# Down projection of a feed-forward layer: two halves over 22 row blocks, or seven half-size products over 11

## Chip, cores and metric

One Trainium2 chip, one of its cores. The metric is the device time of one launch in microseconds (us). Names of engines: PE multiplies matrices and loads its stationary operand (PEld), DVE works on vectors, ACT evaluates functions and copies, POOL is the general engine, which also issues transfers by a queue of its own, and SP issues most transfers. Sums of products stand in PSUM banks of 128 x 512 numbers, everything else that an engine reads in SBUF. DRAM is the memory that transfers read and write.

## Reference

Two decoder layers on 512 tokens of width 1024, all in f32. Each has a mixer (layer 0: forgetting attention and a short convolution; layer 1: a gated linear recurrence, RG-LRU), a cross attention into 256 memory rows, and a gated feed-forward part. Cut to what the change touches:

```python
D_FF = 2816
def swiglu(h, w_gu, w_down):
    g, u = jnp.split(h @ w_gu, 2, axis=-1)
    return (jax.nn.silu(g) * u) @ w_down          # (512 x 2816) @ (2816 x 1024)
for layer in range(2):
    ...                                            # mixer, cross attention
    h = rmsnorm(x, g_ffn_pre[layer])
    y = swiglu(h, w_ffn_gu[layer], w_ffn_down[layer])
    x = x + rmsnorm(y, g_ffn_post[layer])
```

## The kernel before

Every f32 operand of PE is split in two parts of type fp32r, hi (a rounded copy, made by ACT) and lo (the rest, made by DVE: `split_out`), and a product is three products: hi x hi, hi x lo, lo x hi. Tokens stand in four tiles `t` of 128 rows, `x[t]`.

Weights come as tiles `st` of 512 KB from DRAM by SP's queue (pool `wst`, 4 buffers) and are split into `wh` and `wl` (pools `whi` and `wlo`, 4 buffers each). A load waits until DVE has split the tile that had its buffer; a split waits until PE is done with the tile that had the `wh` buffer. So the loads run about eight tiles ahead of PE. Larger arrays are groups of 128 x 2048 numbers (pool `gpool`, 14 buffers).

The feed-forward part `ffn` has three stages. A first pair of columns is made by `ws_gemm_split`, while `hook` ends the sub-layer before (row norms of tiles 2 and 3, transposes). Then `Winograd.stream` makes the gate and up products as seven half-size products for each chunk of 256 columns, 20 chunks. Each pair of chunks gives two row blocks of y = silu(g) * u, which POOL stores in DRAM (`put_y`) from a tile of `wst`. Last comes the down projection (`OutProj` with `nk` = 22 row blocks of 128 of `w_ffn_down`). `half0` makes output columns 0 to 511 for all four token tiles, `half1` columns 512 to 1023; y is loaded back in groups (`load_y`) and split by `parts`, and the last eight row blocks of `half1` run tile by tile, so that `chain` (sum of squares, `rstd` with a power on POOL, gain, add to `x`) and the next row norm of one tile lie beside the products of the next.

Within `Winograd.stream` the programs of PE, DVE, ACT and POOL are the order of the code. In the rest only PE's is, and a scheduler orders the other engines' instructions. SP's is always the scheduler's. Each engine runs its own program strictly in order.

Of the kernel before, what the change touches and what calls it, by code (L numbers as in the profile page):

```python
# [15 lines left out]
P = 128  # L16
# [9 lines left out]
LEAD = 2  # L26
# [8 lines left out]
WHI = 4  # L35
# [7 lines left out]
def trunk_kernel(ctx: ExitStack, tc: tile.TileContext, a: dict, out: bass.AP):  # L43
# [32 lines left out]
    def f(ap):  # L76
        return ap.bitcast(F32)
# [39 lines left out]
    def load_raw(w, k0, nk, c0, c):  # L117
        st = wst.tile([P, nk, c], F32, tag="st", name="st")
        nc.sync.dma_start(
            out=st, in_=w.rearrange("(k p) n -> p k n", p=P)[:, k0:k0 + nk, c0:c0 + c]  # L120
        )
        return st
# [4 lines left out]
    def load_rows(w, k0, n, c0):  # L127
# [5 lines left out]
        return hi, lo  # L133

# [65 lines left out]
    def rstd(st):  # L200
# [9 lines left out]
        nc.gpsimd.tensor_tensor(out=st[:, 4:5], in0=st[:, 3:4], in1=nhalf, op=ALU.pow)  # L210
# [307 lines left out]
    class OutProj:  # L518
        def __init__(self, w, y, nk, g_post, g_pre, hT, first=bankA, second=bankB, final=False):
# [6 lines left out]
            self.ready = {}  # L526
            self.ahead = self.gate = None
# [10 lines left out]
        def half0_steps(self, ks, first, last):  # L538
# [5 lines left out]
            for n, k in enumerate(ks):  # L544
                wt = self.ready.pop(k) if k in self.ready else load_w(self.w, k, 2, 0, 512)
                if self.ahead:
                    for k2 in ks[n + LEAD:n + LEAD + 1]:
                        self.ahead(k2)
# [76 lines left out]

        def run(self):
            self.half0(range(0, self.nk, 2), True, True)
            self.half1()
# [42 lines left out]
    def memory_kv(layer, vhi, vlo, between):  # L671
# [5 lines left out]
        for c in range(4):  # L677
# [8 lines left out]
            split_out(ps, kh_[:, c, :], kl_[:, c, :])  # L686
        between()
# [16 lines left out]
    def cross(layer, hT, kv, proj, hTf):  # L704
# [6 lines left out]
        def q_head(h):  # L711
# [4 lines left out]
            qs[h] = q  # L716

# [76 lines left out]
    def ffn(layer, hT, prev, proj):  # L794
        w = a["w_ffn_gu"][layer]
        y = Feat([None] * NFF, [None] * NFF)

        y2 = dram.tile([P, NFF, 512], F32, name=f"y2_{layer}")
        yraw, yback = {}, {}
# [6 lines left out]
        def put_y(jp):  # L806
            nc.gpsimd.dma_start(out=y2[:, 2 * jp:2 * jp + 2, :], in_=yraw[jp])
# [31 lines left out]
        def load_y(i):  # L839
            n = min(4, NFF - 4 * i)  # L840
            yback[i] = f(group("yb"))
            nc.gpsimd.dma_start(out=yback[i][:, 0:n, :], in_=y2[:, 4 * i:4 * i + n, :])

        def parts(jp):
            if jp // 2 not in yback:
                load_y(jp // 2)
            yg = group("y")
            split_out(yback[jp // 2][:, jp % 2 * 2:jp % 2 * 2 + 2, :], yg[:, 0:2, :], yg[:, 2:4, :])
            for m in range(2):
                y.hi[2 * jp + m], y.lo[2 * jp + m] = yg[:, m, :], yg[:, 2 + m, :]  # L850

        def side(left):

            if left == 3:
                load_y(0)
            if left:
                return {}
            raw = [load_raw(proj.w, k, 2, 0, 512) for k in (0, 2)]
            for i in (1, 2):
                load_y(i)  # L860

            def weights(n):
                proj.ready[2 * n] = split_w(raw[n], 2, 512)

            return {"a": lambda: weights(0), "b": lambda: parts(0), "c": lambda: weights(1), "d": lambda: parts(1)}
# [7 lines left out]
        proj.y = y  # L873
        proj.ahead = lambda k: parts(k // 2)
        proj.run()


    def fox(proj):
# [136 lines left out]
        def qk_pairs(m0):  # L1015
# [12 lines left out]
            yield from ws_steps(w, m0 * P, hT, put_q)  # L1028
            yield from ws_steps(w, FOXW + m0 * P, hT, put_k)

# [73 lines left out]
        def conv(m0):  # L1104
# [30 lines left out]
            yield from ws_steps(w, base + FOXW, hT, put_c)  # L1135
            yield from ws_steps(w, base + 2 * FOXW, hT, put_u)
            yield from ws_steps(w, base, hT, put_b)

# [23 lines left out]
    def rglru(hT, prev, proj):  # L1162
# [70 lines left out]
        conv(0, b0)  # L1233
        conv(1, b1)
        conv(2, ws_gemm(w, D + 512, hT))
        gates(0)
        conv(3, ws_gemm(w, D + 768, hT))
        gates(1)
        gelu(0, ws_gemm(w, 0, hT))
        gates(2)  # L1240
        gelu(1, ws_gemm(w, 256, hT))
        gates(3)
        gelu(2, ws_gemm(w, 512, hT))
        gelu(3, ws_gemm(w, 768, hT))
# [55 lines left out]
```

## Time and profile before

| | |
|---|---|
| median of 3 runs | 1418.07 us (1417.96 to 1418.48) |
| the profiled execution, its own time | 1419.26 us |
| its span, first to last instruction | 1417.5 us, granted clock 0.997 |
| busy | PE 1406.5 us (99%), DVE 1013.9 (72%), ACT 663.6 (47%), POOL 55.9 (4%) |
| moved | 174.34 MB, mean 123 GB/s |
| down projection, first product | 622.6 us in layer 0, about 668.6 us later in layer 1 |

A line of groups reads: line of the code, engine, operation, output <- inputs with sizes, count, busy time and mean duration. A line of the timeline: start, duration, the same names, and in brackets how long the engine sat idle before it and what ended that. Starts are counted from the span's start.

### The profile page before, as it was taken

How to read it: one execution, taken by the hardware profiler on the slowest of the kernel's cores; microseconds unless marked ns; L12 is line 12 of the kernel's file. 1: busy time of each engine (PE TensorE's matmuls, PEld its weight loads, DVE VectorE, ACT ScalarE, POOL GpSimd, SP SyncE). 2: the span in 40 equal slices, each digit the busy share in tenths (PEclk: the TensorE clock that was granted, in tenths of full speed). 3: DMA queues.
4: the chain of work that ended last, by engine and by line, in shares of the span. 5: the costliest groups of instructions: out<-in, count | busy, mean ns of one | idle time of the engine just before them, and what ended most of it. 6: DMA issues, size and time to landing. Idle time of an engine off the chain costs nothing.

```text
span 1417.5 us, 21486 instructions
## 1 busy us (share of the span) xinstructions
PE 1406.5 (99%) x8564; PEld 1252.3 (88%) x8564; DVE 1013.9 (72%) x1623; ACT 663.6 (47%) x1069; POOL 55.9 (4%) x116
## 2 busy tenths in 40 slices
PE   8999999999999999999999999999999999999998
PEld 6778789888899999998889888988889999999886
DVE  5776777635689999992447898754478999998232
ACT  4354455433565444452334896543356444445130
POOL 1000001000000000010000000100000000000000
PEclk9999999999999999999999999999999999999999
DMA  5633152521234434373512336252023334347321
GB/s 175 190 89 99 56 184 83 194 90 45 68 117 144 148 121 138 131 266 120 164 52 82 104 93 198 97 178 89 31 80 114 129 125 147 122 144 272 104 74 60
DMA packets 124287, 174.34 MB, mean 123 GB/s; under 512 B 6725, under 2 KB 88721, under 8 KB 122906
## 3 DMA queue, kind: packets, MB, share of 16 engines
q1 hardware_dynamic: 114722, 140.92, 31.3%
q0 software_dynamic: 5568, 25.18, 4.8%
q10 hardware_dynamic: 3896, 6.86, 1.6%
q8 instruction: 67, 1.10, 0.3%
q14 instruction: 34, 0.28, 0.1%
HBM read 159.29 MB, written 13.65 MB: 122 GB/s over the span
## 4 chain that ended last, share of the span: by engine, by line
PE 99%; DMA 1%; ACT 0%; DVE 0%; DVEq 0%; POOLq 0%; issue 0%; SPq 0%; ACTq 0%
PE bA L299 14%; PE bA L301 14%; PE bA L300 14%; PE bB L300 6%; PE bB L299 6%; PE bB L301 6%; PE bA L534 5%; PE bA L536 5%; PE bA L535 5%; PE bB L535 5%; PE bB L534 5%; PE bB L536 5%; PE bA L905 2%; PE bB L283 1%; PE bA L697 1%; PE bA L699 1%
## 5 line engine op out<-in xcount | busy, mean ns | idle before, releaser
L510 DVE TENSOR_TENSOR wl<-st,wh 128x1024 fp32r<-128x1024 f32 x148 | 180.5, 1223 | 187.8 <-ACT wh L509 186.6
L509 ACT CAST wh<-st 128x1024 fp32r<-128x1024 f32 x148 | 155.3, 1051 | 214.4 <-PE bA L300 66.1
L299 PE MATMUL bA<-hTh,wh 128*128 128x512 f32 (+1 forms) x448 | 171.4, 383 | 0.0
L301 PE MATMUL bA<-hTh,wl 128*128 128x512 f32 (+1 forms) x448 | 168.0, 375 | 0.0
L300 PE MATMUL bA<-hTl,wh 128*128 128x512 f32 (+1 forms) x448 | 167.7, 374 | 0.0
L401 ACT CAST wg<-wr 128x1024 fp32r<-128x1024 f32 x80 | 83.6, 1046 | 49.1 <-DVE wr L430 37.6
L301 PEld LDWEIGHTS bA<-hTh,wl 128*128 128x128 f32 x448 | 84.3, 188 | 15.4
L402 DVE TENSOR_TENSOR wg<-wr,wg 128x1024 fp32r<-128x1024 f32 x80 | 97.4, 1217 | 0.0
L300 PEld LDWEIGHTS bA<-hTl,wh 128*128 128x128 f32 x448 | 84.5, 189 | 13.6
L299 PEld LDWEIGHTS bA<-hTh,wh 128*128 128x128 f32 x448 | 84.5, 189 | 13.5
L534 PE MATMUL bB<-wh,y 128*128 128x512 f32 x208 | 80.9, 389 | 0.0
L535 PE MATMUL bB<-wl,y 128*128 128x512 f32 x208 | 80.9, 389 | 0.0
L536 PE MATMUL bB<-wh,y 128*128 128x512 f32 x208 | 80.9, 389 | 0.0
L401 ACT CAST wh<-tt 128x1024 fp32r<-128x1024 f32 x40 | 42.1, 1052 | 61.2 <-DVE tt L430 61.2
L299 PE MATMUL bA<-hTq,wh 128*128 128x256 f32 x208 | 59.2, 284 | 0.0
L301 PE MATMUL bA<-hTq,wl 128*128 128x256 f32 x208 | 58.9, 283 | 0.0
L300 PE MATMUL bA<-hTq,wh 128*128 128x256 f32 x208 | 58.9, 283 | 0.0
L534 PE MATMUL bA<-wh,y 128*128 128x512 f32 x144 | 56.5, 392 | 0.0
L536 PE MATMUL bA<-wh,y 128*128 128x512 f32 x144 | 56.1, 390 | 0.0
L535 PE MATMUL bA<-wl,y 128*128 128x512 f32 x144 | 56.1, 389 | 0.0
L402 DVE TENSOR_TENSOR wl<-tt,wh 128x1024 fp32r<-128x1024 f32 x40 | 48.7, 1219 | 0.0
L534 PEld LDWEIGHTS bB<-wh,y 128*128 128x128 f32 x208 | 39.1, 188 | 8.1
(330 smaller groups left out, 4171.7 us busy)
## 6 DMA issues: line engine op xcount, KB each, us to landing
wr<-in_w_ffn_gu_dram SPq DMA_DIRECT2D x80, 512.0 KB, 4.6
st<-in_w_ffn_down_dram SPq DMA_DIRECT2D x44, 512.0 KB, 3.9
st<-in_w_xkv_dram SPq DMA_DIRECT2D x32, 512.0 KB, 4.6
st<-in_ab_w_in_dram SPq DMA_DIRECT2D x24, 512.0 KB, 3.8
y<-yr POOLq DMA_DIRECT2D x22, 512.0 KB, 3.9
yb<-y POOLq DMA_DIRECT2D x10, 1024.0 KB, 7.0
st<-in_w_xq_dram SPq DMA_DIRECT2D x16, 512.0 KB, 3.4
st<-in_w_xo_dram SPq DMA_DIRECT2D x16, 512.0 KB, 3.9
```

What stands on the lines that cost most here:

```text
L283: nc.tensor.transpose(out=ps[:, j * P:(j + 1) * P], in_=hs[hf][:, j * P:(j + 1) * P], identity=ident)
L299: nc.tensor.matmul(out=ps, lhsT=wh, rhs=xh, start=first, stop=False)
L300: nc.tensor.matmul(out=ps, lhsT=wh, rhs=xl, start=False, stop=False)
L301: nc.tensor.matmul(out=ps, lhsT=wl, rhs=xh, start=False, stop=last)
L401: return (lambda: nc.scalar.copy(out=to[0], in_=src), lambda: nc.vector.tensor_tensor(out=to[1], in0=src, in1=f(to[0]), op=ALU.subtract))
L402: lambda: nc.vector.tensor_tensor(out=to[1], in0=src, in1=f(to[0]), op=ALU.subtract))
L509: nc.scalar.copy(out=hi, in_=src)
L510: nc.vector.tensor_tensor(out=lo, in0=src, in1=f(hi), op=ALU.subtract)
L534: nc.tensor.matmul(out=ps, lhsT=yh, rhs=wh[:, kk, :], start=first, stop=False)
L535: nc.tensor.matmul(out=ps, lhsT=yh, rhs=wl[:, kk, :], start=False, stop=False)
L536: nc.tensor.matmul(out=ps, lhsT=yl, rhs=wh[:, kk, :], start=False, stop=last)
L905: nc.tensor.matmul(out=banks[t], lhsT=(hT.lo if c == "x" else hT.hi)[k][:, ts], rhs=(wl if c == "w" else wh)[:, kk, :], start=passes[t] == ...
```

## The change

The down projection becomes seven products of half the rows, half the depth and half the columns (a Strassen-Winograd form). The 22 row blocks are taken in pairs: even and odd blocks are the two halves of the depth (11 blocks each, `NJ`), columns 0 to 511 and 512 to 1023 the two halves of the width, tiles 0, 1 and 2, 3 the two halves of the tokens. Each product takes 11 row blocks x 2 token tiles x 3 matmuls of 512 columns, in 6 items (`NG`) of two blocks (the last of one).

The weight sums that four products need (`t1` to `t4`) are made in DRAM. For each layer 16 copies (SP) and 16 adding transfers (POOL, `accum_op`) of up to 786 KB are kept in the list `todo`, and `spend` issues the next few at places in the mixer, the cross attention and the gate and up stage: the copies in the mixer, eight adds in the cross attention, eight in the gate and up stage. The sums of y (`n1`, `n3`, `s2`, `n4`) are made in SBUF by DVE (`sub`), in place in the groups that hold y, one product ahead of their use; `part` splits the 512 numbers a partition that an item needs. The seven results are combined by DVE from the banks (`after`), and `finish` replaces `chain` and `next` in pieces that are set between the items. The whole down projection is now inside the stretch whose order on ACT, DVE and POOL is that of the code. The store of y writes runs of 256 numbers, where it wrote 1024.

```diff
+    todo = []
+    latest = {}
+    def spend(n=1):
+        for _ in range(min(n, len(todo))):
+            engine, step = todo.pop(0)
+            with tc.issue_after(latest[engine]):
+                latest[engine] = step().ins
...
+    class DownProj(OutProj):
+        NJ = NFF // 2
+        NG = (NFF + 3) // 4
+        A = {"a21": 0, "n3": 0, "a11": 1, "s2": 1, "n4": 1, "a22": 2, "n1": 2, "a12": 3}
+        ORDER = (("a11", "b11"), ("a22", "t4"), ("s2", "t2"), ("n3", "t3"), ("n1", "t1"), ("a12", "b21"), ("n4", "b22"))
+        RAW = {"b11": (0, 0), "b12": (0, 1), "b21": (1, 0), "b22": (1, 1)}
+            self.sums = {n: dram.tile([self.NJ * P, 512], F32, name=f"{n}_{layer}") for n in ("t1", "t2", "t3", "t4")}
+            self.y = dram.tile([P, self.NG, 4, 2, 256], F32, name=f"y_{layer}")
...
+            cuts = [(j, min(j + 3, self.NJ)) for j in range(0, self.NJ, 3)]
+            def step(to, frm, js, add):
+                if add:
+                    return nc.gpsimd.dma_start(out=self.rows(to, *js), in_=self.rows(frm, *js), accum_op=ALU.add)
+                return nc.sync.dma_start(out=self.rows(to, *js), in_=self.rows(frm, *js))
+            todo.extend(
+                ("pool" if add else "sp", lambda to=to, frm=frm, js=js, add=add: step(to, frm, js, add))
+                for add, pairs in ((False, (("t1", "b11"), ("t3", "b12"), ("t2", "b11"), ("t4", "b21"))),
+                                   (True, (("t3", "b22"), ("t1", "b12"), ("t2", "t3"), ("t4", "t2"))))
+                for to, frm in pairs for js in cuts
+            )
+        def put_y(self, jp, yr):
+            latest["pool"] = nc.gpsimd.dma_start(out=self.y[:, jp // 2, :, jp % 2, :],
+                                                 in_=yr.rearrange("p m (h c) -> p (m h) c", h=2)).ins
...
+        def sub(self, o, x, y, i):
+            r = self.raw[i]
+            nc.vector.tensor_tensor(out=r[:, self.A[o], :], in0=r[:, self.A[x], :], in1=r[:, self.A[y], :], op=ALU.subtract)
...
+            split_out(src, g[:, i % 2 * 2, 0:n], g[:, i % 2 * 2 + 1, 0:n])
+        def load_b(self, item):
+            (_, name), b = item
+            j0, j1 = 2 * b, min(2 * b + 2, self.NJ)
+            st = wst.tile([P, j1 - j0, 512], F32, tag="st", name="st")
+            nc.sync.dma_start(out=st, in_=self.rows(name, j0, j1))
+            return st
+        def split_b(self, s):
+            st = self.load_b(self.items[s])
+            self.wt[s] = split_w(st, st.shape[1], 512)
...
+        def mms(self, s, ts, banks):
+            (name, _), b = self.items[s]
+            wh, wl = self.wt[s]
+            for jj in range(wh.shape[1]):
+                j = 2 * b + jj
+                g = self.parts[name, b // 2]
+                for t in ts:
+                    cs = slice(jj * 256 + t * P, jj * 256 + t * P + P)
+                    yh, yl = g[:, b % 2 * 2, cs], g[:, b % 2 * 2 + 1, cs]
+                    first, last = j == 0, j == self.NJ - 1
+                    nc.tensor.matmul(out=banks[t], lhsT=yh, rhs=wh[:, jj, :], start=first, stop=False)
+                    nc.tensor.matmul(out=banks[t], lhsT=yh, rhs=wl[:, jj, :], start=False, stop=False)
+                    nc.tensor.matmul(out=banks[t], lhsT=yl, rhs=wh[:, jj, :], start=False, stop=last)
+        def finish(self, t, c):
+            st = self.st[t] = stats("post")
+            def square():
+                for hf in range(2):
+                    sumsq(c[hf], st[:, hf:hf + 1])
+            def gain(hf):
+                nc.vector.tensor_tensor(out=c[hf], in0=c[hf], in1=self.g_post[hf], op=ALU.mult)
...
+            return square, lambda: (gain(0), gain(1)), add, stats_x, root, scale
...
+            for i in range(len(self.raw), N):
+                self.load_y(i)
+            beside = {
+                0: lambda i: (self.part("a22", i), self.sub("n1", "a21", "a22", i)),
+                1: lambda i: (self.sub("n3", "a21", "a11", i), self.sub("s2", "a11", "n1", i), self.part("s2", i)),
+                2: lambda i: (self.part("n3", i), self.sub("n4", "a12", "s2", i)),
+                3: lambda i: self.part("n1", i),
+                4: lambda i: self.part("a12", i),
+                5: lambda i: self.part("n4", i),
+            }
+            p1, q, v, c21 = ([g[:, 2 * h + t, :] for t in range(2)] for g in (g1, g2) for h in range(2))
+                if x_ == 0:
+                    return [lambda t=t: nc.scalar.copy(out=p1[t], in_=bk[t]) for t in range(2)]
...
+                if x_ == 2:
+                    return [lambda t=t: tt(q[t], bk[t], p1[t], ALU.subtract) for t in range(2)]
+                if x_ == 3:
+                    return [lambda t=t: (tt(v[t], bk[t], q[t], ALU.add), tt(c21[t], C["p4"][t], v[t], ALU.subtract))
+                            for t in range(2)]
+                if x_ == 4:
+                    return [lambda t=t: (tt(v[t], bk[t], v[t], ALU.add), tt(q[t], bk[t], q[t], ALU.add)) for t in range(2)]
+                if x_ == 5:
+                    return [lambda t=t: tt(p1[t], bk[t], p1[t], ALU.add) for t in range(2)]
...
+            for t in range(2):
+                steps = self.finish(t, (c21[t], v[t]))
+                if self.final:
+                    steps = steps[:3]
+                else:
+                    steps += lambda t=t: self.transpose(t, bankB),
+                for n, fn in enumerate(steps):
+                    at = 5 * N + 1 + t + n
+                    extra.setdefault((at // N, at % N), []).append(fn)
...
+                if s + 2 < len(self.items) and s + 2 not in self.wt:
+                    self.split_b(s + 2)
+                if x_ == 0 and b + 2 < N:
+                    self.part("a11", b + 2)
+                if x_ in beside:
+                    beside[x_](b)
+                if b in (1, 2) and pend:
+                    pend.pop(0)()
+                for fn in extra.get((x_, b), ()):
+                    fn()
+                if x_ < 6 or b < N - WHI:
+                    self.mms(s, (0, 1), bk)
+                if b == N - 1 and x_ < 6:
+                    pend = after(x_, bk)
...
+            for t in range(2):
+                for s2 in range(len(self.items) - WHI, len(self.items)):
+                    self.mms(s2, (t,), bk)
+                tt(q[t], bk[t], q[t], ALU.add)
+                sq, ga, ad, st, ro, sc = self.finish(2 + t, (p1[t], q[t]))
+                sq()
+                ga()
+                for fn in last:
+                    fn()
+                ad()
+                if t == 0 and not self.final:
+                    st()
+                    ro()
+                    last = [sc]
...
+            proj.begin()
+            for i in (1, 2, 3):
+                proj.load_y(i)
+            return {"a": lambda: proj.split_b(0), "b": lambda: proj.part("a11", 0),
+                    "c": lambda: proj.split_b(1), "d": lambda: proj.part("a11", 1)}
...
```

Not shown: `spend` is called after each of four column groups of `memory_kv`, after each head of `cross`, at every second chunk of the gate and up stage (one step each), and twice at a time between the products of the mixers. The final stores of tiles 0 and 1 go to POOL's queue.

DVE's order where the gate and up stage of layer 0 ends and the down projection begins. Before (`wl` is the lo part of a weight tile, `y` that of two row blocks of y):

```order
L831 TENSOR_TENSOR yr_6336<-yr_6336,sw_6215 128x512
L510 TENSOR_TENSOR wl_6436<-st_6433,wh_6435 128x1024
L510 TENSOR_TENSOR y_6439<-yb_6251,y_6439 128x1024
L510 TENSOR_TENSOR wl_6469<-st_6466,wh_6468 128x1024
L510 TENSOR_TENSOR y_6472<-yb_6251,y_6472 128x1024
L510 TENSOR_TENSOR wl_6502<-st_6499,wh_6501 128x1024
L510 TENSOR_TENSOR y_6507<-yb_6505,y_6507 128x1024
L510 TENSOR_TENSOR y_6540<-yb_6505,y_6540 128x1024
L510 TENSOR_TENSOR y_6575<-yb_6573,y_6575 128x1024
```

Now, in the first product. `wl` is the weight tile two items ahead, `ya` the lo parts of the first and second product's y blocks, and the operation on `yb` alone the sum `n1`:

```order
L1044 TENSOR_TENSOR yr_6374<-yr_6374,sw_6251 128x512
L520 TENSOR_TENSOR wl_6428<-st_6425,wh_6427 128x1024
L520 TENSOR_TENSOR ya_6431<-yb_6283,ya_6431 128x512
L520 TENSOR_TENSOR ya_6434<-yb_5920,ya_6434 128x512
L685 TENSOR_TENSOR yb_5920<-yb_5920 128x512
L520 TENSOR_TENSOR wl_6453<-st_6450,wh_6452 128x1024
L520 TENSOR_TENSOR ya_6431<-yb_6285,ya_6431 128x512
L520 TENSOR_TENSOR ya_6434<-yb_6281,ya_6434 128x512
L685 TENSOR_TENSOR yb_6281<-yb_6281 128x512
L520 TENSOR_TENSOR wl_6476<-st_6473,wh_6475 128x1024
L520 TENSOR_TENSOR ya_6479<-yb_6415,ya_6479 128x512
```

Where DVE had one or two splits for each of 11 weight tiles of a half, each item now has four operations. In the second product these are a weight split, two sums (`n3` and `s2`, in one row), and the lo part of `s2`, whose hi part ACT makes from the sum just made:

```order
L685 TENSOR_TENSOR yb_6417<-yb_6417 128x256
L520 TENSOR_TENSOR wl_6563<-st_6560,wh_6562 128x1024
L685 TENSOR_TENSOR yb_5920<-yb_5920 128x512 x2
L520 TENSOR_TENSOR ya_6568<-yb_5920,ya_6568 128x512
L520 TENSOR_TENSOR wl_6586<-st_6583,wh_6585 128x1024
L685 TENSOR_TENSOR yb_6281<-yb_6281 128x512 x2
L520 TENSOR_TENSOR ya_6568<-yb_6281,ya_6568 128x512
L520 TENSOR_TENSOR wl_6609<-st_6606,wh_6608 128x1024
L685 TENSOR_TENSOR yb_6283<-yb_6283 128x512 x2
L520 TENSOR_TENSOR ya_6614<-yb_6283,ya_6614 128x512
```

POOL's order from the last row norm of layer 0's mixer on. Before, with the power operations of the norms (`post`, `pre`) and the first stores of y:

```order
L210 TENSOR_TENSOR pre_3543<-pre_3543,nhalf_108 128x1
L210 TENSOR_TENSOR post_3340<-post_3340,nhalf_108 128x1
L210 TENSOR_TENSOR pre_3646<-pre_3646,nhalf_108 128x1
L807 DMA y2_0_3577<-yr_3906 128x1024
L807 DMA y2_0_3577<-yr_4107 128x1024
L807 DMA y2_0_3577<-yr_4355 128x1024
L807 DMA y2_0_3577<-yr_4603 128x1024
L807 DMA y2_0_3577<-yr_4851 128x1024
```

Now eight adds stand behind the mixer's last norm and ahead of the cross attention's first, with nothing between them:

```order
L220 TENSOR_TENSOR pre_2208<-pre_2208,nhalf_108 128x1
L663 DMA t3_0_121<-in_w_ffn_down_dram 128x3x512 x3
L663 DMA t3_0_121<-in_w_ffn_down_dram 128x2x512
L663 DMA t1_0_119<-in_w_ffn_down_dram 128x3x512 x3
L663 DMA t1_0_119<-in_w_ffn_down_dram 128x2x512
L220 TENSOR_TENSOR post_3366<-post_3366,nhalf_108 128x1
L220 TENSOR_TENSOR pre_3456<-pre_3456,nhalf_108 128x1
L220 TENSOR_TENSOR post_3367<-post_3367,nhalf_108 128x1
L220 TENSOR_TENSOR pre_3514<-pre_3514,nhalf_108 128x1
L220 TENSOR_TENSOR post_3368<-post_3368,nhalf_108 128x1
```

130 lines of the change are left out of this document (90 added, 40 removed).

## Prediction

> **What bounds the kernel now.** I read the page's busy times first, then the chain of waits, then the stages one by one.
>
> ```profile
> PE 1406.5 (99%) x8564; PEld 1252.3 (88%) x8564; DVE 1013.9 (72%) x1623; ACT 663.6 (47%) x1069; POOL 55.9 (4%) x116
> PE 99%; DMA 1%; ACT 0%; DVE 0%; DVEq 0%; POOLq 0%; issue 0%; SPq 0%; ACTq 0%
> ```
>
> PE has work for 1406.5 of 1417.5 us, and the chain that ended last is PE almost throughout. So a matmul taken away is worth its full place in PE's row, until another engine or a transfer is late. The stages, by a table of windows (length, busy times, granted clock, DMA share, GB/s):
>
> ```profile
> core 0: us, PE busy (x) PEld busy (x) DVE busy (x) ACT busy (x) POOL busy (x), PEclk, DMA share, GB/s
> 64.00:130.00 66.00, 66.00 (x350) 52.12 (x349) 45.46 (x107) 32.43 (x66) 4.19 (x9) 1.00 0.36 104
> 240.00:264.00 24.00, 24.00 (x184) 23.12 (x183) 16.66 (x19) 12.29 (x16) 0.00 (x0) 1.00 0.61 199
> 264.00:300.00 36.00, 36.00 (x160) 29.81 (x159) 16.50 (x17) 13.80 (x17) 0.00 (x0) 1.00 0.46 146
> 424.00:604.00 180.00, 180.00 (x1501) 179.85 (x1500) 170.55 (x270) 81.81 (x107) 5.39 (x10) 1.00 0.40 135
> 622.00:640.00 18.00, 18.00 (x84) 15.02 (x83) 16.62 (x16) 9.94 (x11) 1.61 (x3) 1.00 0.88 318
> 640.00:680.00 40.00, 40.00 (x179) 33.10 (x178) 9.80 (x8) 7.62 (x8) 0.00 (x0) 1.00 0.31 99
> ```
>
> The reader sees a steady down projection (640 to 680) in which PE is full while DVE has 9.8 of 40 us and the transfers a third of their time: there is room for more vector work and more bytes. Its first 18 us are the opposite: DVE 16.6 of 18 us, DMA engines 0.88 busy at 318 GB/s.
>
> **What is removed: 132 matmuls.** Two halves x 22 blocks x 4 tiles x 3 = 528 matmuls a layer become 7 x 11 x 2 x 3 = 462, of the same form (stationary 128 x 128, 512 columns). A matmul's duration of 389 ns overlaps the next one, so the price is the distance of starts. The first row is from the list of y's readers, the other two are PE's timeline, 15 matmuls apart:
>
> ```profile
> L534 PE MATMUL bB<-wh,y x208: 389/389/396, 622.6 to 1350.4; 128*128 128x512 f32 x104
> 639.62 0.39 PE L534 MATMUL bB<-wh,y 128*128 128x512 f32 x1
> ...
> 643.02 0.39 PE L534 MATMUL bB<-wh,y 128*128 128x512 f32 x1
> ```
>
> (643.02 - 639.62) / 15 = 0.2267 us; 132 x 0.2267 = **29.9 us gained**. Not 132 x 0.389 = 51, which would count the overlap. An item of two blocks (12 matmuls) now takes PE 2.72 us, a product 14.96.
>
> **DVE in the first two products: 5.2 us lost a layer.** Prices of DVE's operations, again as distances of starts, at the end of the gate and up stage (the 512-wide operations are the same kind as a sum or the lo part of half an item), and ACT's cast of 512:
>
> ```profile
> 621.53 0.42 DVE L830 TENSOR_TENSOR yr<-bA,wy 128x256 f32<-128x256 f32 x1
> 621.87 1.22 DVE L510 TENSOR_TENSOR y<-yb,y 128x1024 fp32r<-128x1024 f32 x1
> 623.00 0.68 DVE L831 TENSOR_TENSOR yr<-yr,sw 128x512 f32<-128x512 f32 x1
> 623.60 0.69 DVE L830 TENSOR_TENSOR yr<-bA,wy 128x512 f32<-128x512 f32 x1
> 624.20 1.22 DVE L510 TENSOR_TENSOR y<-yb,y 128x1024 fp32r<-128x1024 f32 x1
> 625.34 0.69 DVE L831 TENSOR_TENSOR yr<-yr,sw 128x512 f32<-128x512 f32 x1
> 607.20 0.61 ACT L401 CAST wh<-t 128x512 fp32r<-128x512 f32 x1
> ```
>
> The last y of that stage on its way through DRAM, and one hand-over from ACT to DVE:
>
> ```profile
> 626.32 0.54 POOL L807 DMA_DIRECT2D y<-yr  x1 [7.05 <-DVE yr L831]
> 626.89 0.54 POOL L842 DMA_DIRECT2D yb<-y  x1
> 630.27 0.54 POOL L842 DMA_DIRECT2D yb<-y  x1 [2.85 <-DMA y<-yr]
> 633.97 1.05 ACT L509 CAST y<-yb 128x1024 fp32r<-128x1024 f32 x1 [4.39 <-DMA yb<-y]
> 635.05 1.23 DVE L510 TENSOR_TENSOR y<-yb,y 128x1024 fp32r<-128x1024 f32 x1 [1.08 <-ACT y L509]
> 637.39 1.05 ACT L509 CAST y<-yb 128x1024 fp32r<-128x1024 f32 x1 [0.46 <-DMA yb<-y]
> ```
>
> DVE's prices: 256 wide 0.34, 512 wide 0.60, 1024 wide 1.14. An item of the first product: a weight split and three of 512, 1.14 + 3 x 0.60 = 2.94 us. In the second product the lo part waits for ACT, which waits for the sum just made: 0.69 + 0.61 and two hand-overs of 0.03 (633.97 + 1.05 to 635.05), less the 0.60 already counted, is 0.76 idle, so 3.70. Third product 2.34, fourth 1.74. PE needs 2.72. With the short sixth items the first product takes DVE 3 x 2.94 + 2.14 + 2.34 + 1.81 = 15.1, the second up to its fifth item 4 x 3.70 + 3.16 = 18.0.
>
> DVE starts on this at 624.0 (PE begins at 622.6; two operations for the last y, 0.60 each, stand ahead). The y groups 4 and 5 can only be loaded then. Before, each such load landed 7.1 us after its issue, and the store took 3.9. The last store now goes out at 624.1 (2.2 earlier, since nothing is put between), group 4 lands at 631.8, group 5 at 635.1, and ACT's cast adds 0.6 and 0.5. DVE reaches their lo parts at 631.0 and, pushed, at 634.8, and waits 1.4 + 0.8 = 2.2. The split that the second item of the third product needs ends at 624.0 + 15.1 + 2.2 + 18.0 + 1.1 = 660.4; PE wants it at 622.6 + 2 x 14.96 + 2.72 = 655.2. That is the 5.2, **10.4 in two layers**, in four or five waits of at most 2.3. From there DVE is cheaper than PE and gets ahead again. Bounds: 0 (no idle for ACT and no y wait: 654.4), and 9 a layer (y 4 us later, as ACT's wait of 4.39). I take the sum itself.
>
> **End of the products.** The prices come from the last chain of the program and one row norm:
>
> ```profile
> 1410.72 0.39 PE L536 MATMUL bA<-rh,y 128*128 128x512 f32 x1
> 1411.92 0.16 DVE L206 SCALAR_TENSOR_TENSOR post<-post 128x1 f32<-128x1 f32 x1 [3.14 <-ACT junk L198]
> 1412.23 0.55 POOL L210 TENSOR_TENSOR post<-post,nhalf 128x1 f32<-128x1 f32 x1 [4.89 <-DVE post L206]
> 1412.81 0.75 DVE L602 SCALAR_TENSOR_TENSOR x<-ya,post,x 128x512 f32<-128x512 f32 x1
> 1413.48 0.75 DVE L602 SCALAR_TENSOR_TENSOR x<-yb,post,x 128x512 f32<-128x512 f32 x1
> ```
>
> Adding a tile to x costs DVE 0.9 until POOL answers and 2 x 0.67. In layer 0 the transposes of tiles 0 and 1 stand on PE ahead of the second and third item of the seventh product. Ahead of the first of them DVE has, from the sixth product's second item on, five splits (5.2), four parts (2.1), combinations (2.4), gains (2.4), two adds (4.6), a part, a root and a scaling (2.2): 18.9 us, against PE's 14.96 + 2.72 = 17.7. PE waits 1.2, then some 0.9 for tile 1: **2 us** (0 to 4). At the border of the layers tile 2's scaled rows come at +3.2 us (0.6 + 1.2 + 1.3 and hand-overs), the transposes after 24 matmuls of 256 columns, at half of 0.2267 each +2.7: **0.5** (0 to 2). At the end of the program the combination (0.7) and two gains (1.2) stand ahead of the row at 1411.92: 1413.0, **1.1** (0.7 to 2). Layer 1's tiles 0 and 1 wait for nobody.
>
> **The sums in DRAM.** No transfer of this kind, DRAM to DRAM or adding, is in the trace. The nearest rows:
>
> ```profile
> yb<-y POOLq DMA_DIRECT2D x10, 1024.0 KB, 7.0
> y<-yr POOLq DMA_DIRECT2D x22, 512.0 KB, 3.9
> 239.23 0.55 POOL L210 TENSOR_TENSOR pre<-pre,nhalf 128x1 f32<-128x1 f32 x1 [2.63 <-DVE pre L206]
> 379.86 0.55 POOL L210 TENSOR_TENSOR post<-post,nhalf 128x1 f32<-128x1 f32 x1 [140.08 <-DVE post L206]
> 484.16 0.53 POOL L807 DMA_DIRECT2D y<-yr  x1 [19.63 <-DVE yr L831]
> 242.39 0.37 SPq L119 DMA_DIRECT2D st<-in_w_xkv_dram  x1
> 251.53 1.05 ACT L509 CAST wh<-st 128x1024 fp32r<-128x1024 f32 x1 [0.39 <-PE bA L300]
> ```
>
> The full rate is 318 / 0.88 = 361 GB/s. POOL is idle for 140 us after the mixer's last norm, so the eight adds there go out at once at 240: 5.8 MB written, twice that read; counted as two plain bytes each 11.5 MB, 32 us of all engines. The loads beside it run at 199 GB/s, a tile of 512 KB in 2.6 us. A load issued at 242.39 is split at 251.53, and with four `wh` buffers a split stands three tiles ahead of PE: 9.1 + 7.8 = 17 us, of which a landing takes 3.9, so 13 are spare. If the loads keep half the rate (180) they lose 2 us in 24; with a third (120) 79 x 40 = 3.2 MB, 16 us, three more than are spare. I take **1 us a layer, 2 in all**, nearer to the half. Ends: 0 (an add takes nothing away, so no gain) and 19 a layer (adds served first, 32 less 13). The eight later adds have 20 us each (the row at 484.16) in a stage whose share is 0.40, and I cost them at nothing; adds of over 20 us each would queue up there, and the sums of the second product would be late.
>
> The copies in the mixers (11.5 MB a layer, counted once: the same 32 us) lie in a stage whose share is 0.36 in 66 us. I cost them at nothing for the weight loads (SP's place eight tiles ahead hides them), but one pair meets the first attention's `cb`:
>
> ```profile
> 71.56 0.29 DVE L1059 CUSTOM_DVE_ANT_0 p<-bB,cb 128x128 f32<-128x128 f32 x1 [4.21 <-DMA cb<-cum]
> 82.86 0.44 PE bB L1078 x4
> ```
>
> DVE already waits there 4.21 us for a transfer, and in the chain of waits PE's transposes of these probabilities come at 82.86, so little lies between: **1 us** (0 to 5). The store of y in runs of 1 KB instead of 4 has 20 us; nothing.
>
> Sum: -29.9 + 10.4 + 2 + 0.5 + 1.1 + 2 + 1 = -12.9; a span of 1404.6. The profiled execution has a span of 1417.5 and a time of 1419.26; the median of the runs is 1418.07, 0.6 over the span: **1405 us**.
>
> [...]
>
> **Rivals.** (B) DVE's waits are covered: the hi part of `s2` is made early enough, y lands sooner. Then the 10.4 shrinks to 0 to 3: 1393 to 1399. For it: the gate and up stage runs with DVE at 95% and PE never waits. Against it: the row at 633.97. Chance 0.16. (C) The adds hold up the loads, and it is slower: at 240 to 280 us, and again 669 us later, the loads get a small part of the DMA engines. From 8 us more a layer than I count the gain is gone; fully served first it is 18 more each: 1421 to 1441. For it: an add's speed is unknown, and all eight stand in one burst. Against: shares of 0.61 and 0.46 there, 13 us spare. [...] Chance 0.16. (D) DVE becomes the bound of the whole down projection: its work there is 44 (splits) + 23 (parts) + 13 (sums) + 8 (combinations) + 14 (ends) = 102 of PE's 104.7 us, so every wait for POOL or a bank that is not covered shows. With 4 to 7 us more a layer: 1413 to 1420. Chance 0.15. (E) The matmuls come out slower than 0.2267 in the new order: the form is the same; 0.02, counted with D. (A) My forecast, 1400 to 1411, has the rest, 0.51.
>
> **Numbers.** Within 0.2% is 1415.2 to 1420.9, about what a measurement of this kernel can tell from no change. Faster: A 0.51, B 0.16, a third of D and E 0.06 = 0.73. Same: 0.09 of D, 0.01 of C = 0.10. Slower: C 0.15, D 0.02 = 0.17. The range 1393 to 1428 takes in B, D and the near part of C and leaves out about 0.15.
>
> **What would show it.** Right: 132 fewer matmuls at 0.2267; waits of PE for DVE's `wl` in the second product and the start of the third, some 5 us, and none in products four to six; PE waiting 2 us for transposes in the seventh product of layer 0. Wrong: ACT's or DVE's weight splits waiting for `st` at 240 to 290 (C), DVE over 95% busy after the third product with PE waiting (D), PE full throughout (B). A landing time of the adds over 20 us each would break the sum in the cross attention first.

## The result, and the profile after

The changed kernel takes 1450.38 us (median of 4, 1449.27 to 1451.52) against 1418.28 for the one before: ratio 1.0225, 95% interval 1.0208 to 1.0243. The forecast was 1405, with 1428 as the upper end. The page and the waits of PE (for whom, us in total, times, longest), then windows of the same columns as before:

```profile
PE 1401.4 (97%) x8432; PEld 1232.0 (85%) x8432; DVE 1120.2 (77%) x1801; ACT 717.9 (50%) x1175; POOL 106.9 (7%) x152
PE 78%; DMA 7%; DVE 7%; issue 5%; ACT 2%; POOL 0%; POOLq 0%; DVEq 0%; ACTq 0%; SPq 0%
PE bB L293 <- DVE h L246: 9.5, 4, 4.5
PE bB L721 <- DVE wl L520: 7.1, 10, 1.1
PE bA L913 <- DVE wl L520: 6.4, 9, 0.8
```

```profile
64.00:84.00 20.00, 16.88 (x82) 12.13 (x81) 8.79 (x29) 6.27 (x16) 1.99 (x5) 0.91 0.59 189
264.00:280.00 16.00, 14.72 (x60) 10.76 (x59) 7.85 (x11) 6.63 (x9) 0.00 (x0) 1.00 1.10 262
280.00:300.00 20.00, 16.32 (x65) 11.85 (x66) 10.43 (x12) 9.18 (x11) 0.00 (x0) 1.00 0.97 264
672.00:675.00 3.00, 0.74 (x3) 0.38 (x3) 2.16 (x3) 1.50 (x2) 0.00 (x0) 0.96 0.42 156
675.00:678.00 3.00, 3.00 (x8) 2.33 (x9) 2.03 (x4) 1.56 (x2) 0.00 (x0) 0.50 0.48 163
741.00:747.00 6.00, 1.79 (x9) 1.79 (x10) 5.34 (x10) 3.21 (x6) 2.41 (x2) 0.67 0.41 132
764.00:770.00 6.00, 2.16 (x15) 1.98 (x15) 5.50 (x10) 1.72 (x6) 0.68 (x2) 0.74 1.02 320
```

The 132 matmuls are gone (8564 to 8432), yet PE's busy time fell by 5.1 us only, and PE's share of the last chain went from 99 to 78%. PE now idles in four kinds of places: the first attention, the cross attention's loads (DMA engines full, shares of 1.10 and 0.97), the second product (DVE's splits late), and the end of the down projection of layer 0. In the windows at 675 and 741 the granted clock is 0.50 and 0.67: PE is "busy" there at half speed. How late PE is against the kernel before is read at matmuls that both have, and in the down projection as time beyond 0.2267 us a matmul between these rows (first and last matmul of each layer's):

```profile
635.02 0.40 PE L720 MATMUL bB<-wh,ya 128*128 128x512 f32 x1
761.29 0.39 PE L722 MATMUL bB<-wh,ya 128*128 128x512 f32 x1
1322.96 0.40 PE L720 MATMUL bB<-wh,ya 128*128 128x512 f32 x1
1441.70 0.39 PE L722 MATMUL bB<-wh,ya 128*128 128x512 f32 x1
```

461 starts at 0.2267 are 104.5 us; layer 0 takes 126.3 (21.8 over), layer 1 takes 118.7 (14.2 over). In the kernel before, layer 0's down projection is 1.8 over, for transposes that lie in it, and layer 1's is not. The forecast's terms beside what the trace shows, as PE's growing lateness against the kernel before:

| step | forecast, us | trace, us |
|---|---|---|
| 132 matmuls fewer | -29.9 | -29.9 |
| copies against the first attention's `cb` | +1 | +4.7 |
| burst of eight adds, both layers | +2 | +7.8, +7.5 |
| products one to three, both layers | +10.4 | +12.0, +11.7 |
| layer 0, last product and border of the layers | +2.5 | +14.8 |
| layer 1, last product | 0 | +2.5 |
| end of the program | +1.1 | +1.2 |
| sum | -12.9 | +32.3 |

The spans differ by 1449.7 - 1417.5 = 32.2, the same but for rounding.

### The profile page after: what moved, and what is told of

Its sections match the earlier page's. It is cut to its first block, busy times and chain, and to the rows that moved or that the text cites. A ratio compares the mean times of both kernels' runs of the same rounds, so it can differ in the third digit from the quotient of the medians.

```text
span 1449.7 us, 21767 instructions
## 1 busy us (share of the span) xinstructions
PE 1401.4 (97%) x8432; PEld 1232.0 (85%) x8432; DVE 1120.2 (77%) x1801; ACT 717.9 (50%) x1175; POOL 106.9 (7%) x152
## 3 DMA queue, kind: packets, MB, share of 16 engines
q0 software_dynamic: 17664, 49.30, 14.8%
## 4 chain that ended last, share of the span: by engine, by line
PE 78%; DMA 7%; DVE 7%; issue 5%; ACT 2%; POOL 0%; POOLq 0%; DVEq 0%; ACTq 0%; SPq 0%
PE bA L309 12%; PE bA L311 12%; PE bA L310 12%; PE bB L310 5%; PE bB L309 5%; PE bB L311 5%; DVE wl L520 3%; DMA st<-in_w_xkv_dram 2%; PE bA L543 2%; PE bA L545 2%; PE bB L545 2%; PE bB L543 2%; PE bA L544 2%; DMA st<-in_w_xq_dram 2%; PE bB L544 2%
## 5 line engine op out<-in xcount | busy, mean ns | idle before, releaser
L520 DVE TENSOR_TENSOR wl<-st,wh 128x1024 fp32r<-128x1024 f32 x196 | 231.4, 1184 | 132.4 <-ACT wh L519 129.3
L519 ACT CAST wh<-st 128x1024 fp32r<-128x1024 f32 x196 | 199.5, 1019 | 191.6 <-PE bA L310 51.7
L721 PE MATMUL bB<-wl,ya 128*128 128x512 f32 x176 | 70.4, 400 | 7.2 <-DVE wl L520 7.1
L720 PE MATMUL bB<-wh,ya 128*128 128x512 f32 x176 | 70.6, 401 | 3.2 <-ACT ya L519 1.7
L519 ACT CAST ya<-yb 128x512 fp32r<-128x512 f32 (+1 forms) x84 | 48.0, 581 | 49.4 <-DVE yb L685 33.4
L722 PE MATMUL bB<-wh,ya 128*128 128x512 f32 x176 | 69.4, 394 | 0.0
L520 DVE TENSOR_TENSOR ya<-yb,ya 128x512 fp32r<-128x512 f32 (+1 forms) x84 | 53.6, 644 | 15.4 <-ACT ya L519 15.2
L720 PE MATMUL bA<-wh,ya 128*128 128x512 f32 x132 | 53.3, 404 | 3.0 <-ACT wh L519 3.0
L721 PE MATMUL bA<-wl,ya 128*128 128x512 f32 x132 | 53.6, 406 | 1.6 <-DVE wl L520 1.6
L722 PE MATMUL bA<-wh,ya 128*128 128x512 f32 x132 | 52.9, 401 | 0.0
## 6 DMA issues: line engine op xcount, KB each, us to landing
st<-in_w_xkv_dram SPq DMA_DIRECT2D x32, 512.0 KB, 13.2
```

The lines of the kernel that those rows point to most:

```text
L519: nc.scalar.copy(out=hi, in_=src)
L520: nc.vector.tensor_tensor(out=lo, in0=src, in1=f(hi), op=ALU.subtract)
L720: nc.tensor.matmul(out=banks[t], lhsT=yh, rhs=wh[:, jj, :], start=first, stop=False)
L721: nc.tensor.matmul(out=banks[t], lhsT=yh, rhs=wl[:, jj, :], start=False, stop=False)
L722: nc.tensor.matmul(out=banks[t], lhsT=yl, rhs=wh[:, jj, :], start=False, stop=last)
```

## Experiments

All times are medians of four or more executions, but for the two kernels on PE's clock; the changed kernel is at 1450.4.

**The burst of adds left out**

```diff
-  ("pool" if add else "sp", ...)
+  (None if add and to in ("t1", "t3") else "pool" if add else "sp", ...)   # spend skips None
```

> Left out in both layers: the eight adds that go out in one burst at the start of the cross attention (t3 += b22, t1 += b12), so the sums are incomplete. The copies and the eight later adds stay. Theory: the burst takes the DMA engines from the loads of w_xkv, which land after 13 us in place of 4.9, and PE falls behind by 7.9 us (layer 0) and 6.9 us (layer 1) in that stage. Without it these 14.8 us come back: about 1435.6 us, loads of w_xkv at about 5 us, PE full from 250 to 300 us. Rival: these loads are late because of their place in SP's queue or because the copies before them moved the stage: time stays at 1450, loads still late. Second rival: adds cost more than their bytes and the eight left in the gate and up stage hurt too; then the gain here is under half of 14.8.

1434.7 us, 15.7 less, with sums that are incomplete. The median landing of the loads of `w_xkv` goes from 13.2 to 5.1 us and PE is full from 240 to 300. The theory holds.

**The same transfers as plain copies, and the adds spread**

```diff
-  accum_op=ALU.add)
+  **({} if to in ("t1", "t3") else {"accum_op": ALU.add}))
```

> The eight transfers of the burst are made as plain copies by the same queue, with the same bytes written and the same places, so that t3 and t1 hold one block and not a sum. Theory: an adding transfer moves its bytes once more (it reads what it adds to) but is otherwise like a copy; as copies the burst asks the engines for about half to two thirds of the time, and of the 14.8 us some 8 to 12 come back: 1438 to 1443 us. Rival: an add goes at a copy's price: 1450 us. Second rival: adding itself is what is slow, and plain copies cost nothing there: 1435 us.

1440.4, with `t1` and `t3` holding one block and no sum: ten of the 15.7 us come back, as expected. From 240 to 300 us, the queue (packets, MB, share of 16 engines) and the loads (count, KB, us to landing), first with adds:

```profile
q0 software_dynamic: 2944, 5.77, 53.8%
st<-in_w_xkv_dram SPq DMA_DIRECT2D x8, 512.0 KB, 14.1
```

and as copies:

```profile
q0 software_dynamic: 1536, 5.77, 28.3%
st<-in_w_xkv_dram SPq DMA_DIRECT2D x8, 512.0 KB, 15.6
```

The same 5.77 MB take 0.538 x 60 = 32.3 us of all engines as adds, 17.0 as copies. About a third of the price is left for half the engine time, though the loads land no sooner (15.6 us against 14.1): the shorter burst is over sooner after the lead of the loads is used up. From 280 to 300 us PE is busy for all 20 us there, and for 16.32 with the adds.

```diff
+  def spend_after(src):
+      g = tiny.tile([P, 1], F32, ...)
+      latest["pool"] = nc.gpsimd.tensor_tensor(out=g, in0=src, in1=nhalf, op=ALU.mult).ins
+      spend()
-  spend()                      # four times in memory_kv, four in q_head
+  spend_after(...)             # q of three heads, pT of the last, each head's output
```

> All 32 transfers of the sums are kept. The eight adds of the burst go out one by one over the cross attention: ahead of each stands a 128 x 1 multiplication on POOL that reads a tile just made (the heads' q, the transposed probabilities, the attention's output), so that POOL waits for that place. Theory: it is the burst that costs, since eight adds at once take the DMA engines for 46 us from a stage that needs 193 GB/s; one add in about 12 us fits beside the loads, so the 14.8 us come back as with the eight left out: 1434 to 1437 us. Rival: an add costs PE the same wherever it lies in the cross attention (its bytes have to go beside loads that run at a share of 0.4 to 0.6): 1443 to 1450 us.

1437.4: 13.0 of the 15.7 are back with every sum complete. The rival (the same price anywhere) falls. What is missing lies at the end of the cross attention, where PE falls 2.0 us (layer 0) and 1.6 us (layer 1) behind the kernel without these adds. The last add goes out at 374.21, and a weight load beside it comes late. ACT's cast waits for it (0.4 us at most at this place without the adds), and the row norm and PE's transposes stand behind:

```profile
383.00 1.05 ACT L525 CAST wh<-st 128x1024 fp32r<-128x1024 f32 x1 [3.01 <-DMA st<-in_w_ffn_gu_dram]
391.53 1.32 PE L299 MATMUL bA<-ident,h 128*128 128x128 f32 x8 [1.53 <-DVE h L252]
```

```profile
t<-in_w_ffn_down_dram POOLq DMA_DIRECT2D x6, 768.0 KB, 8.8
```

This last line is an add's landing from 300 to 400 us there, 8.8 us; in the burst the median was 23.3.

**Copies kept off the first attention**

```diff
  yield from ws_steps(w, m0 * P, hT, put_q)
- spend(m0)
...
  yield from proj.half0_steps((4, 6), True, False)
+ spend(2)
```

> Layer 0 alone: the pair of copies that SP issues at 66.7 us, just ahead of the first attention's cb loads, is issued after the attention instead (with its later pairs one place on). Theory: the two copies (786 KB each) hold up cb, and PE loses 4.6 us at 74 to 77 us to it: 1445.8 us. Rival: cb is late because other copies (of 56.9 us) are still under way, or because POOL issues it late: 0 to 1 us less.

1446.5, 3.9 less, near the theory. The window of the attention, to be held against the one above (PE 16.88 of 20, clock 0.91):

```profile
64.00:84.00 20.00, 20.00 (x104) 15.01 (x103) 11.46 (x37) 8.91 (x22) 2.76 (x6) 1.00 0.43 138
```

**s2 cast one item later**

```diff
- 1: (sub n3(i), sub s2(i), part s2(i)),        2: (part n3(i), sub n4(i)),
+ 1: (part s2(i - 1), sub n3(i), sub s2(i)),    2: (i == 0: part s2(N - 1); part n3(i), sub n4(i)),
```

> One change: in the second product both casts of s2 (hi on ACT, lo on DVE) are made one item after the sum s2, not in the same item; the last one goes to the first item of the third product. Theory: DVE and ACT wait for each other once an item there (DVE makes s2, ACT casts it and only then the next weight, DVE waits for both), 4.2 us an item in place of 2.94; without the waits the splits for the third product come 6 to 7 us earlier, PE waits about 5 us a layer in place of 11.8 and keeps its full clock: about 13 us less, 1437 us. Rival: the first two products are bound by DVE's amount of work and the late landing of y, not by the order: at most 3 us less, 1447 to 1450.

1434.8, 15.5 less. DVE in the changed kernel, one item of the second product, and what ACT does meanwhile:

```profile
665.63 1.23 DVE L520 TENSOR_TENSOR wl<-st,wh 128x1024 fp32r<-128x1024 f32 x1 [0.74 <-ACT wh L519]
666.78 1.41 DVE L685 TENSOR_TENSOR yb<-yb 128x512 f32<-128x512 f32 x2
668.88 0.69 DVE L520 TENSOR_TENSOR ya<-yb,ya 128x512 fp32r<-128x512 f32 x1 [0.69 <-ACT ya L519]
669.88 0.69 DVE L520 TENSOR_TENSOR wl<-st,wh 128x512 fp32r<-128x512 f32 x1 [0.31 <-ACT wh L519]
```

```profile
668.22 0.62 ACT L519 CAST ya<-yb 128x512 fp32r<-128x512 f32 x1 [2.62 <-DVE yb L685]
668.75 0.58 ACT L783 COPY c<-bB 128x512 f32<-128x512 f32 x1
669.23 0.62 ACT L519 CAST wh<-st 128x512 fp32r<-128x512 f32 x1
```

DVE waits twice an item: for the hi part of `s2`, and then for the next weight's hi part, which stands behind that cast in ACT's row. 665.63 to 669.88 is 4.25 us. With the cast an item later:

```profile
657.89 1.22 DVE L520 TENSOR_TENSOR wl<-st,wh 128x1024 fp32r<-128x1024 f32 x1
659.02 0.68 DVE L520 TENSOR_TENSOR ya<-yb,ya 128x512 fp32r<-128x512 f32 x1
659.62 1.41 DVE L685 TENSOR_TENSOR yb<-yb 128x512 f32<-128x512 f32 x2
660.95 1.22 DVE L520 TENSOR_TENSOR wl<-st,wh 128x1024 fp32r<-128x1024 f32 x1
```

3.06 us, without a wait. The rival (DVE's amount of work) falls.

**The transposes at the end of layer 0, three times**

```diff
- steps += lambda t=t: self.transpose(t, bankB),     # ahead of items 2 and 3 of product seven
+ (after the last four items of tile 0, and of tile 1: self.transpose(t, bankB))
+ hook: transpose(2) at block 2, transpose(3) at block 3 of the next stage (were 0 and 2)
```

> Layer 0 alone: the transposes of tiles 0 and 1 come after the last four items of the seventh product for tile 0 and for tile 1, not ahead of its second and third item, and the transposes of tiles 2 and 3 come after the third and fourth block of 24 matmuls of the next stage, not after the first and third. Theory: PE's 6.3 us and 3.9 us waits there are the row norms' chain (DVE, ACT, POOL, DVE) which PE's order asks for too early, and each wait of over 3 us is followed by some 3 us at half clock; with the later places the waits shrink to about 2.5 us (the first matmul of layer 1 after the transposes of tile 1): 11 to 12 us less, 1439 us. Rival: DVE's total work bounds this stretch, and the same wait stands at the next place: 0 to 4 us less, 1446 to 1450.

1452.0: nothing gained, 1.6 more, and the theory failed as I had put it. The half clock that it counts on stands behind the two waits of PE of over 3 us that the changed kernel's trace has: 4.50 us until 745.21, with starts 0.4267 us apart behind the transposes until 749.9, and 3.84 us until 769.01, with starts of 256 columns 0.2133 us apart until 773.7. The wait at the old place is gone, but the first matmul of layer 1 now waits:

```profile
764.23 0.58 PE L309 MATMUL bA<-hTh,wh 128*128 128x256 f32 x1 [4.53 <-ACT hTh L302]
```

```profile
762.98 0.63 ACT L208 ACTIVATE junk<-c 128x512 bf16<-128x512 f32 x1 [0.63 <-DVE c L765]
763.61 1.05 ACT L302 CAST hTh<-bB 128x512 fp32r<-128x512 f32 x2
```

ACT's cast of tile 1's transposes stands in its row behind tile 3's squares, which wait for DVE. So the next kernel sets tile 0's transposes after item 2 of product seven and tile 1's after tile 0's last items. It stands on four edits, which were run together first (spread adds, copies off `cb`, later casts, and the fifth y group loaded before the last y's store):

> Four edits together: the adds spread, s2 cast one item later, the copies kept off the first attention's cb, and the fifth group of y loaded before the last y is stored (it holds none of it). Theory: the losses are separate and add up: 1450.4 - 15 - 15.5 - 3.9 = 1416, and up to 2 us more a layer for the y group (PE waited 0.3 + 0.9 + 1.4 us for it and for what stands behind it on DVE): 1412 to 1416 us. Rival: two of them hide one another, and the sum stays above 1420.

1418.1 us, ratio 0.9998 (0.9988 to 1.0007): the losses add up (1450.4 less 13.0, 3.9 and 15.5 is 1418.0), which leaves nothing for the y group, and so it is 2 us above the range. No run has the y group alone. Then, with the transposes placed as said:

> The kernel with the four edits and later transposes, but n4's casts at their old place in the sixth product. It tells apart what the 9.8 us between the four edits and that kernel come from. Theory: PE's order asks for the transposed rows too early, and DVE is also short of time; each of the two edits gives a part, so this one lies between, 1411 to 1415 us. Rival: DVE's work is all of it: 1417 to 1419 us, no gain without the earlier casts. Second rival: the places of the transposes are all of it: 1408 to 1409 us.

1410.0 us, 8.1 less. And with n4's casts begun three items earlier as well:

> The four edits, and at the end of the down projection: n4's casts begin three items earlier (in the fifth product), the transposes of tile 0 stand after the second item of the seventh product and those of tile 1 after tile 0's last four items, and in layer 1 the transposes of tiles 2 and 3 come after the third and fourth block of 24 matmuls. With the transposes alone moved to the very end nothing was gained, since ACT's cast of the transposes then stood behind the next row norm and DVE had work without a break from 728 to 768 us. Theory: DVE's work in the sixth and seventh product is the bound (18 us of it between its first combination and tile 0's scaled rows, where PE takes 13); 2 to 4 us of it moved ahead, and PE asked later, take away most of the 6.3 us wait, its 1.6 us of half clock and about half of the 3.9 us at the border: 8 us less than the four edits alone, 1404 to 1408 us. Rival: the wait moves on to the first matmuls of layer 1: within 3 us of the four edits.

1408.4 us. So the places of the transposes are 8.1 of the 9.7 us; the 1.6 for DVE's work lie about at what the medians can tell. The theory that DVE's work is the bound does not hold for most of it. Of the middle kernel's forecasts both the second rival (1408 to 1409) and the theory (1411 to 1415) missed by 1 us, the rival the nearer in kind.

**The late y**

```diff
- if x_ == 0 and b + 2 < N: part a11(b + 2)
+ if x_ == 0 and b + 2 < N - 1: part a11(b + 2)
+ if s == N - 2: part a11(N - 1)              # behind split_b(s + 2)
```

> The fastest kernel so far (1408.4 us), and in the first product the casts of y's last group stand on ACT and DVE one item later, behind the weight split of the second product's first item. Theory: DVE sits in front of the late y while the split behind it is what PE wants next (gaps of 1.4 us in layer 0 and 0.65 us in layer 1 at the second product's first wl); in the other order they go: 1406.5 us. Rival: PE then waits for the y group itself by as much: no difference, 1408.4 us.

1404.65 us, ratio to the kernel before 0.9906 (0.9889 to 0.9923), span 1401.9: faster than both. The gain, 3.7, is twice what the two gaps would give. By one trace of each kernel (their own times are 4.2 us apart) it lies in products one to three: they take 5.4 us (layer 0) and 2.7 us (layer 1) beyond 0.2267 a matmul without this edit and 3.0 and 1.05 with it. In the second and third of them the 1.4 and 2.6 us that were lost shrink to 0.1 each, so the splits there come in time as well.

```profile
PE 1380.9 (99%) x8432; PEld 1225.8 (87%) x8432; DVE 1118.1 (80%) x1801; ACT 719.4 (51%) x1175; POOL 110.6 (8%) x168
```

**PE's clock**

```diff
+ for _ in range(45):      # then 75; ahead of tile 0's transposes
+     nc.tensor.matmul(out=ps[:, 0:P], lhsT=identb, rhs=mask, start=True, stop=True)
```

> The changed kernel, with 45 small bf16 matmuls (128 columns, result not used) ahead of the transposes of tile 0 in the seventh product of layer 0, where PE waits 4.5 us. Theory: the matmuls at 0.4267 us that follow this wait are the granted clock at 0.5 after idle time; with PE busy in most of the wait the matmuls behind it start 0.2267 us apart at once, the granted clock stays 1.0 in 747 to 750 us, and the time is up to 1.6 us less. Rival: the slow matmuls come from late operands or from contention at that place, and stay at 0.4267 us.

A miss: 45 took 2.69 us, 2.0 us of idle time were left, and the clock still fell, for half as long.

> As the kernel with 45 small matmuls, with 75. The 45 took 2.69 us and left PE idle for 2.0 us, and the granted clock still fell to 0.5, from 745.3 to 748.7 us, half as long as without them (743.5 to 749.6 us). [...]

The choice is the one of the run with 45: idle time, or late operands and contention at that place. The windows behind the wait, with no fillers, with 45 and with 75. In the first two pairs the rows are the first and the last with a lowered clock, from which its bounds follow (0.51 is half clock for 0.98 of that microsecond): 743.0 to 749.9 us with none, 745.3 to 748.8 with 45.

```profile
743.00:744.00 1.00, 0.00 (x0) 0.00 (x0) 0.96 (x1) 0.65 (x1) 1.00 (x1) 0.51 0.71 217
749.00:750.00 1.00, 1.00 (x4) 0.75 (x4) 1.00 (x3) 0.00 (x0) 0.00 (x0) 0.57 0.96 331
```

```profile
745.00:746.00 1.00, 1.00 (x6) 0.86 (x4) 1.00 (x2) 0.86 (x3) 1.00 (x1) 0.67 0.45 157
748.00:749.00 1.00, 1.00 (x5) 0.77 (x4) 1.00 (x3) 0.00 (x0) 0.00 (x0) 0.62 0.65 228
```

```profile
744.00:746.00 2.00, 1.62 (x19) 1.24 (x16) 1.88 (x5) 0.41 (x1) 0.15 (x2) 1.00 0.58 185
746.00:748.00 2.00, 2.00 (x12) 1.66 (x11) 2.00 (x3) 1.71 (x3) 1.31 (x1) 1.00 0.24 79
```

With 75 the clock stays at 1.00 and the matmuls behind the transposes start 0.23 us apart at once. The border's wait of 3.84 us, which has no fillers, is still followed by half clock in that run (0.50 from 768 to 770 us). So at this place it is PE's idle time that halves the clock, by one execution of each kernel. (Their times, 1450.1 and 1448.9, can't show the 1.6 us at stake.)

## Why the prediction was wrong, step by step

- **Matmuls (-29.9).** Right: in steady stretches the starts are 0.2267 us apart. That the kernel with all the edits lands at 1404.65, near the forecast, is luck: 29.9 us less would be 1388.4, and the 16 us lost there are not those of the sum (of its 10.4 for products one to three 4.0 are left).
- **The burst (+2, was +15.3).** Rival (C)'s mechanism. My sum of the adds' engine time, 32 us, was right (32.3). The step that failed is "13 us are spare", with the choice of half the rate for the loads. A tile of 512 KB in 3.99 us is 131 GB/s, near the third (120) for which I had 3 us a layer; 7.8 and 7.5 were lost. The lead exists once; after it each `st` buffer must come round in time. Four buffers at a landing of 14.1 us bring a tile about every 4 us. That is what ACT and PE show, ACT waiting for the load and PE 3.99 us from tile to tile where it needs 2.72:

```profile
282.34 1.05 ACT L519 CAST wh<-st 128x1024 fp32r<-128x1024 f32 x1 [2.94 <-DMA st<-in_w_xkv_dram]
280.71 0.50 PE L913 MATMUL bA<-wl,mTh 128*128 128x512 f32 x1 [0.77 <-DVE wl L520]
284.70 0.50 PE L913 MATMUL bA<-wl,mTh 128*128 128x512 f32 x1 [0.77 <-DVE wl L520]
```

  4 x 3.99 less 14.1 leaves 1.9 us in which ACT and DVE hold the buffer, so by this estimate the loads may land after 4 x 2.72 - 1.9 = 9.0 us at most, once the lead is spent. That was to be asked, and the bound of 0 to 19 a layer held the answer.
- **`cb` (+1, was +4.7).** Right in kind and inside its bounds (0 to 5); I took the low end though the row showed DVE waiting already. 3.1 us are PE's wait, most of the rest is half clock behind it.
- **Products one to three (+10.4, was +23.7).** Right place, too small. The step that failed is the 3.70 us an item: it was 4.2, mostly because I counted ACT's hi part of `s2` but not the weight cast queued behind it on ACT; and y's last two groups came 1.4 and 2.6 us later than I had them (645.6 and 650.1, where 631.8 and 635.1 plus the 12.4 us of lag give 644.2 and 647.5). The last store of y, at 636.93, had landed by 642.73, after 5.8 us where I had 3.9; why, no run shows. Late y and slower items share the miss about equally: in layer 0 DVE comes to the second product's items 3.1 us later than my sum has it and loses 3.1 more in them.
- **End of layer 0 (+2.5, was +14.8).** The step that failed is to set DVE's 18.9 us against PE's 17.7 from the same start. PE starts the sixth product at 721.79. DVE can't be early: its split at 721.71 waits for a `wh` buffer that PE frees (ACT's cast at 720.63), so it comes to the second item at 723.46, 1.7 us after PE. From there tile 0's scaled rows take 22.4 us, not 18.9. Six splits stand in DVE's row where I counted five (1.1 us). ACT's cast for the one at 727.67 is 1.20 us late, behind a square that waits for DVE's own combination, and 0.44 goes at POOL's power. The first half of the rows is there at 745.2, PE asks at 740.7, and so again for tile 2 at the border (by PE's lateness 8.0 us lie ahead of the last matmul, 6.8 behind it):

```profile
720.63 1.05 ACT L519 CAST wh<-st 128x1024 fp32r<-128x1024 f32 x1 [1.36 <-PE bB L722]
721.71 1.23 DVE L520 TENSOR_TENSOR wl<-st,wh 128x1024 fp32r<-128x1024 f32 x1 [1.16 <-ACT wh L519]
727.67 1.23 DVE L520 TENSOR_TENSOR wl<-st,wh 128x1024 fp32r<-128x1024 f32 x1 [1.20 <-ACT wh L519]
745.21 1.97 PE L293 MATMUL bB<-ident,h 128*128 128x128 f32 x8 [4.50 <-DVE h L246]
769.01 1.94 PE L293 MATMUL bB<-ident,h 128*128 128x128 f32 x8 [3.84 <-DVE h L246]
```

- **No term for the clock.** Half clock shows as starts 0.4267 us apart behind the waits (0.2133 for matmuls of 256 columns, which start 0.12 apart else). These add 1.4 us behind `cb`'s wait, 1.5 in product seven of layer 0 and 1.3 at the border: some 4 of the 45 us missed. In the third products they add 1.2 and 2.2, but little of it is lost, since PE has to wait there for DVE's splits in any case: in layer 0 it still waits 0.33 us for one at 682.44. In layer 1 the kernel with 75 fillers, which stand in layer 0 alone, has the same waits at the start of that product (1.5 us, and starts 1.25 apart behind it) and yet the full clock, and takes 18.3 us for it where the changed kernel takes 18.7. First the changed kernel, then the one with 75:

```profile
1362.00:1364.00 2.00, 1.89 (x5) 1.50 (x6) 1.35 (x3) 0.58 (x2) 0.00 (x0) 0.50 0.31 81
1360.00:1362.00 2.00, 2.00 (x9) 1.66 (x10) 1.28 (x3) 0.79 (x2) 0.00 (x0) 1.00 0.44 108
```

  Around the wait of 4.50 us the clock was low for 6.9 us, and for 3.5 us where 45 fillers left a wait of 1.99 us; at 672 to 675 it fell though no single wait was over 1.5 us, with PE busy for 0.74 of 3.0 us. So the longest single wait does not decide it. Nor does the idle time of such a stretch alone, as the two rows above show; no run here gives the rule.

Of what was costed at nothing, the later adds, the stores of y during the gate and up stage and the copies in layer 1's mixer held up nothing: PE's lateness stays at 12.4 us from 420 to 629 and at 24.2 from 775 to 955. The last product of layer 1 cost 2.5, in two waits for DVE's splits (0.78 us at 1425.62, 1.12 at 1429.78).

The burst and `cb` lay inside their bounds, products one to three (9 a layer) and the end of layer 0 (4 + 2) above theirs. All four missed to the same side, by some 43 us, and the range had 23 above the forecast: room for any one of them and not for all.

## What to carry to other kernels

A prefetch lead is spent once: test a burst by buffers over landing time against the consumer's pace (here four at 14.1 us against 2.72 us a tile), and spread background transfers by an instruction that waits for the place where you want them. Where two engines hand work to and fro within one item, count what is queued behind the handed piece on both, and move the consumer an item later (here 4.25 us an item became 3.06). PE waits of 3.1, 3.84 and 4.50 us were followed here by 1.3 to 1.5 us lost to half clock. And the place where PE's order asks for a result was cheaper to move than DVE's work was to shrink (8.1 us against 1.6).

## Not expected of the hardware

An adding transfer from DRAM to DRAM took 1.9 times the engine time of a copy of the same bytes (32.3 against 17.0 us for 5.77 MB). And POOL's power on 128 x 1 took 1.63 us where it ran beside a split of DVE that began in the same moment, and 0.55 where DVE was idle (at 769.87):

```profile
742.74 1.63 POOL L220 TENSOR_TENSOR pre<-pre,nhalf 128x1 f32<-128x1 f32 x1 [3.32 <-DVE pre L216]
742.74 1.23 DVE L520 TENSOR_TENSOR wl<-st,wh 128x1024 fp32r<-128x1024 f32 x1
```

Of the 52 powers in this trace five took 1.41 to 1.63 us, and each of the five ran beside a split of 128 x 1024 on DVE. The other 47 took 0.54 to 0.56 us, 17 of them beside a DVE operation of 512 columns and none beside a split. Why, no run shows.
